# Strassen's seven products in the input projections of three feed-forward layers

## The chip, the cores and the metric

The kernel runs on one core of a Trainium2 chip. The metric is the device time of one execution in microseconds; the lower, the better. Three runs of the kernel before took 3054.96, 3058.57 and 3060.85 us.

## The reference

A network over 512 tokens of width 1024, all in float32. A first block has two layers of mixed recurrent and sparse attention; a second block has two layers, each with a feed-forward network, a mixer, cross-attention to a memory and another feed-forward network. The change is in the feed-forward networks of the second block, four in all:

```
def swiglu_ffn(x, w_in, w_out):
    h = x @ w_in                      # [512, 1024] @ [1024, 5632]
    g, u = jnp.split(h, 2, axis=-1)
    return (jax.nn.silu(g) * u) @ w_out   # [512, 2816] @ [2816, 1024]
...
for i in range(DEPTH):                # 2
    x = layer_norm(a * x + 0.5 * swiglu_ffn(x, ffn_w_in[i, 0], ffn_w_out[i, 0]), ...)
    h = diff_attention(x, ...)  if i == 0 else pool_mixer(x, ...)
    x = layer_norm(a * x + h, ...)
    x = layer_norm(a * x + memory_cross_attention(x, mem, ...), ...)
    x = layer_norm(a * x + 0.5 * swiglu_ffn(x, ffn_w_in[i, 1], ffn_w_out[i, 1]), ...)
```

## The kernel before, in words

The activations stay in the chip's memory: X holds the residual stream with tokens on the partitions, xT (tiles xh and xl) holds it with features on the partitions. Every float32 operand of a matrix product is kept as two parts, an upper one rounded to the matmul's format and a lower one, the rest. A product is three matmuls (upper times upper, upper times lower, lower times upper): `mm3`, L169.

Weights come in units of 512 KB. `units` (L146) loads a unit into a staging tile `wst` (three buffers) with a DMA from SP's queue, ScalarE copies it to the upper part `whi` (L151), and VectorE subtracts that from the staging tile to get the lower part `wlo` (L155). whi and wlo have six buffers each.

`ffn` (L1093) computes one feed-forward layer. The 2816 hidden features are 22 tiles of 128, here called u, worked on in chunks, by default two of 11. For each u there are two units of `w_in`, one for the gate (PSUM tile g, three buffers) and one for the other half (PSUM tile a, two buffers). Each takes 8 row tiles x 3 matmuls with 512 moving columns, the tokens. ScalarE then takes Silu of the gate, VectorE multiplies, ScalarE and VectorE split h into hh and hl (L1121 to L1124). After a chunk comes its share of the output projection, in two halves of 512 output columns, for four tiles of 128 tokens; VectorE adds each result to X (L1138). In the last chunk, for the second half of the columns, the work goes token tile by token tile: matmuls, addition, statistics, layer norm (`ln_tile`, L264, with a power on GpSimd, L198), and the transposition of the tile before into the next xT (`x_T`, L278).

The first two u of a layer are computed in two token halves of 256, since the last token tile of xT comes late: the first half for both, then `flush` (the transposition of the last tile that the phase before left over), then the second half.

The four layers are called at L1623, L1632, L1636 and L1654. The third call asks for chunks of 8, 7 and 7 and carries the pool mixer's steps along. Instructions stand in each engine's queue in an order that the framework fixes when the program is built: it starts from the order of the program text and may put an instruction that it expects to be ready ahead of one that it expects to wait. Waits between engines are by semaphores that it adds.

Of the kernel before, what the change touches and what calls it, by code (L numbers as in the profile page):

```python
# [45 lines left out]
def constants():  # L46
    """Arrays that depend on shapes alone."""
# [38 lines left out]
class Net:  # L86
# [43 lines left out]

    def raw(s, key, *parts):
        """Parts of the weight: the rows r0*128.. (nk tiles of 128) and the columns cols, float32."""
        st = s.w.tile([128, UN], F32, name="wst", bufs=3)
        ap = s.d[key]
        at = 0
        for idx, r0, nk, cols in parts:
            n = nk * len(cols)
            s.specs.setdefault(key, []).append((idx, r0, nk, cols))
            off = s.woff.get(key, 0)
            s.woff[key] = off + 128 * n  # L140
            s.nc.sync.dma_start(st[:, at:at + n], bass.AP(tensor=ap.tensor, offset=ap.offset + off,
                                                          ap=[[n, 128], [1, n]]))
            at += n
        return st, at

    def units(s, key, *parts):  # L146
        """hi and lo of the parts of the weight, each [128, nk, columns]."""
        st, n = s.raw(key, *parts)
        hi = s.w.tile([128, UN], F32R, name="whi", bufs=6)
        lw = s.w.tile([128, UN], F32R, name="wlo", bufs=6)  # L150
        s.nc.scalar.activation(hi[:, :n], st[:, :n], AF.Copy)  # L151
        if s.lo_pool:
            s.nc.gpsimd.tensor_sub(lw[:, :n], st[:, :n], hi[:, :n])
        else:
            s.nc.vector.tensor_sub(lw[:, :n], st[:, :n], hi[:, :n])  # L155
# [5 lines left out]
        return out  # L161

# [11 lines left out]
    def split_ps(s, hi, lo, ps, scale=None):  # L174
        """hi + lo = ps (times a power of two)."""
# [8 lines left out]
    def split_q(s, dst, ps, scale=1.0):  # L184
        """Queries of pairs of heads, feature-major in ps [2 * 64, pairs, tokens], to dst [hi; lo], a head at a time."""
# [6 lines left out]
    def rsqrt(s, v, n, scale, eps, p=128, post=None):  # L192
        """(v * scale + eps) ** -0.5, elementwise on [p, n]."""
# [39 lines left out]
    def to_T(s, src, t, k0, dst):  # L233
        """src [128 tokens, 4 * 128] -> hi / lo [128, k0..k0+3, tokens of tile t]."""
# [6 lines left out]
    def rms_tile(s, t, G, junk):  # L241
        """rmsnorm of X[:, t]."""
        return s.rms_scale(t, G, junk, s.rms_stats(t, junk))
# [20 lines left out]
    def ln_tile(s, t, ST, G, B, parts=1, out=None):  # L264
        """X[:, t] <- layer_norm(sqrt(2) * X[:, t]) with the stats of X in ST."""
# [12 lines left out]
    def x_T(s, t):  # L278
        """X[:, t] feature-major, hi / lo, into s.xT."""
# [4 lines left out]
    def fm(s, key, idx, cols, halves=False, ps=None):  # L284
        """One tile of 128 features, feature-major: [128, 512 tokens] in PSUM."""
# [29 lines left out]
    def tm(s, xT, us, t, ps, ks=None):  # L315
        """Token-major product of the tokens of tile t with the units: [128 tokens, columns] in PSUM."""
# [20 lines left out]
    def open_norm(s, i):  # L337
        """What the first norm of the block takes, on the right side."""
# [167 lines left out]
    def ple(s, i, P):  # L506
        """p @ w_pp / 2 into DRAM, in eight pieces."""
# [26 lines left out]
    def hgrn(s, i, H, L, yh, hf):  # L534
        """The projections; returns the events of the four heads: eight slots a head, and a tail."""
# [262 lines left out]
    def compress(s, i, N, K, gates):  # L798
        """Compressed keys (transposed, twice over the partitions) and block-diagonal values:
# [925 lines left out]
```

## Time and profile before

| | |
|---|---|
| median of three runs | 3058.57 us |
| profiled execution, first to last instruction | 3057.3 us |
| TensorE matmuls busy | 2979.0 us, 15502 instructions |
| VectorE busy | 1656.9 us |
| ScalarE busy | 1144.0 us |
| GpSimd busy | 434.4 us |
| moved by DMA | 296.66 MB |

The profile is one execution on the chip. A busy matmul row counts each matmul from its start to its modelled end, and matmuls overlap, so the pace of a series is read from the starts. A wait is put down to the instruction that ended it last. "PEclk" is the granted clock of TensorE as a share of full speed, "DMA" the mean busy share of the core's 16 DMA engines.

### The profile page before, as it was taken

The page shows a single profiled execution, that of the slowest core. Times are in us where ns is not written, and L with a number is a line of the kernel's source. Part 1 is how long each engine was busy: PE and PEld are TensorE (multiplying, and loading weights), DVE is VectorE, ACT ScalarE, POOL GpSimd, SP SyncE. Part 2 cuts the span into 40 slices and gives each one's busy share as a digit, 9 for nine tenths or more (in the row PEclk, how much of TensorE's full clock was granted, in tenths as well). Part 3 has the DMA queues.
Part 4 walks back from the last instruction along what each step waited for, and adds up shares of the span by engine and source line. Part 5 has one row for each costly group of instructions (what it writes and reads, how often), then busy time and mean ns, then how long its engine had stood idle before and what let it go on. Part 6 is the DMA issues. An engine that isn't in the chain of part 4 may idle for free.

```text
span 3057.3 us, 39959 instructions
## 1 busy us (share of the span) xinstructions
PE 2979.0 (97%) x15502; PEld 2501.9 (82%) x15502; DVE 1656.9 (54%) x2813; ACT 1144.0 (37%) x2063; POOL 434.4 (14%) x555
## 2 busy tenths in 40 slices
PE   8989999989999999999999999999999999999999
PEld 7778778878788888888888888888888888888887
DVE  5676855786765323378775633335333386643334
ACT  6445636545633222245544332222222224332221
POOL 1553500563410000011100000000000040000000
PEclk9999999999999999999999999999999999999999
DMA  5213134113133232231143232324322224132321
GB/s 186 70 55 104 41 128 162 56 61 102 46 121 120 93 100 97 87 107 60 59 157 121 88 104 90 100 90 136 104 97 95 92 75 148 68 118 90 100 91 65
DMA packets 94141, 296.66 MB, mean 97 GB/s; under 512 B 12416, under 2 KB 18048, under 8 KB 93952
## 3 DMA queue, kind: packets, MB, share of 16 engines
q1 hardware_dynamic: 93808, 293.85, 29.5%
q8 instruction: 122, 2.00, 0.3%
q14 instruction: 67, 0.55, 0.1%
q10 hardware_dynamic: 144, 0.26, 0.0%
HBM read 281.49 MB, written 12.58 MB: 96 GB/s over the span
## 4 chain that ended last, share of the span: by engine, by line
PE 82%; DVE 10%; ACT 3%; issue 2%; DMA 2%; POOL 1%; SPq 0%; DVEq 0%; ACTq 0%; POOLq 0%
PE g L167 56%; PE a L167 19%; PE o L167 4%; DVE wlo L155 2%; PE t L237 1%; PE t L1060 1%; POOL rs_y L198 1%; DVE X L274 1%; DVE nb L946 0%; DVE PTl L179 0%; ACT whi L151 0%; DMA wst<-in_w_in 0%; DVE xl L179 0%; DVE AT L645 0%; DVE dqst L190 0%
## 5 line engine op out<-in xcount | busy, mean ns | idle before, releaser
L151 ACT ACTIVATE whi<-wst 128x1024 fp32r<-128x1024 f32 (+1 forms) x478 | 495.9, 1039 | 1173.2 <-PE g L167 453.5
L155 DVE TENSOR_TENSOR wlo<-wst,whi 128x1024 fp32r<-128x1024 f32 (+2 forms) x471 | 572.6, 1220 | 646.5 <-ACT whi L151 627.1
L167 PE MATMUL g<-xh,whi 128*128 128x512 f32 (+1 forms) x1296 | 478.5, 370 | 2.8 <-ACT xh L178 2.2
L167 PE MATMUL g<-xl,whi 128*128 128x512 f32 (+1 forms) x1296 | 476.6, 368 | 1.1 <-DVE xl L179 1.0
L167 PE MATMUL g<-xh,wlo 128*128 128x512 f32 (+1 forms) x1296 | 475.4, 367 | 0.0
L198 POOL TENSOR_TENSOR rs_y<-rs_a,mhalf 128x1 f32<-128x1 f32 (+4 forms) x90 | 100.1, 1113 | 2119.9 <-DVE rs_a L197 2118.4
L167 PE MATMUL g<-whi,xh 128*128 128x512 f32 (+2 forms) x960 | 365.9, 381 | 0.0
L167 PE MATMUL g<-wlo,xh 128*128 128x512 f32 (+2 forms) x960 | 359.5, 374 | 0.8 <-DVE wlo L155 0.8
L167 PE MATMUL g<-whi,xl 128*128 128x512 f32 (+2 forms) x960 | 359.2, 374 | 0.0
L167 PE MATMUL a<-xl,whi 128*128 128x512 f32 (+1 forms) x768 | 286.2, 373 | 0.0
L167 PE MATMUL a<-xh,wlo 128*128 128x512 f32 (+1 forms) x768 | 285.5, 372 | 0.0
L167 PE MATMUL a<-xh,whi 128*128 128x512 f32 (+1 forms) x768 | 285.2, 372 | 0.0
L167 PEld LDWEIGHTS g<-xh,whi 128*128 128x128 f32 x1296 | 244.5, 189 | 43.5 <-ACT xh L178 3.4
L167 PEld LDWEIGHTS g<-xl,whi 128*128 128x128 f32 x1296 | 244.6, 189 | 39.7 <-DVE xl L179 1.5
L167 PEld LDWEIGHTS g<-xh,wlo 128*128 128x128 f32 x1296 | 244.3, 189 | 39.9 <-DVE wlo L155 0.5
L167 PE MATMUL g<-whi,hh 128*128 128x512 f32 x568 | 224.8, 396 | 0.0
L167 PE MATMUL g<-whi,hl 128*128 128x512 f32 x568 | 224.5, 395 | 0.0
L167 PE MATMUL g<-wlo,hh 128*128 128x512 f32 x568 | 224.4, 395 | 0.0
L1122 DVE TENSOR_TENSOR h<-h,a 128x512 f32<-128x512 f32 x88 | 60.6, 688 | 279.8 <-PE a L167 277.7
L167 PEld LDWEIGHTS g<-whi,xl 128*128 128x128 f32 x960 | 182.6, 190 | 30.7
L167 PEld LDWEIGHTS g<-wlo,xh 128*128 128x128 f32 x960 | 183.1, 191 | 29.5 <-DVE wlo L155 1.4
L167 PEld LDWEIGHTS g<-whi,xh 128*128 128x128 f32 x960 | 182.9, 191 | 28.1
(363 smaller groups left out, 4847.4 us busy)
## 6 DMA issues: line engine op xcount, KB each, us to landing
wst<-in_ffn_w_in SPq DMA_DIRECT2D x176, 512.0 KB, 3.5
wst<-in_ffn_w_out SPq DMA_DIRECT2D x80, 512.0 KB, 3.5
wst<-in_w_in SPq DMA_DIRECT2D x64, 512.0 KB, 4.0
wst<-in_xa_wkv SPq DMA_DIRECT2D x32, 512.0 KB, 3.6
wst<-in_da_w_qkv SPq DMA_DIRECT2D x24, 512.0 KB, 3.9
wst<-in_w_out SPq DMA_DIRECT2D x16, 512.0 KB, 3.5
wst<-in_w_pg SPq DMA_DIRECT2D x16, 512.0 KB, 4.4
wst<-in_xa_wq SPq DMA_DIRECT2D x16, 512.0 KB, 4.4
```

The lines of the kernel that those rows point to most:

```text
L151: s.nc.scalar.activation(hi[:, :n], st[:, :n], AF.Copy)
L155: s.nc.vector.tensor_sub(lw[:, :n], st[:, :n], hi[:, :n])
L167: s.nc.tensor.matmul(out, lhsT, rhs, start=start, stop=stop)
L198: nc.gpsimd.tensor_tensor(y, a, s.mhalf[:p].to_broadcast([p, n]), op=OP.pow)
L237: s.nc.tensor.transpose(ps[:, j], src[:, j * 128:(j + 1) * 128], s.ident)
L274: nc.vector.scalar_tensor_tensor(X[:, cs], X[:, cs], rs, B[:, cs], op0=OP.mult, op1=OP.add)
L1060: nc.tensor.transpose(pt[:, j], me["P"][:, j * 128:(j + 1) * 128], s.ident)
L1122: nc.vector.tensor_mul(h, h, pu)
```

## The change

In three of the four layers (both of the first network layer and the last one) the hidden features from u = 2 on are taken in pairs of tiles. For a pair, gate and other half are each 256 columns wide, so `w_in` for it is a 2 x 2 arrangement of blocks (gate or other half, upper or lower 512 rows), and xT is a 2 x 2 arrangement (upper or lower 512 features, first or second 256 tokens). Instead of eight block products there are seven, of sums of blocks, in Strassen's and Winograd's form.

- `sums` makes, once a layer, the four sums of blocks of x on VectorE, and splits them into upper and lower parts (ScalarE and VectorE). It uses three or four of the staging tiles.
- `seven_units` makes the seven weight operands of a pair. Three are blocks as they are. Four are sums: a block is loaded by SP's queue into one of four tiles `sq`, and a second block, or a sum made before, is added by a DMA from GpSimd's queue that accumulates into the tile. s2 takes s3 as its source, s4 takes s2.
- `products` computes the seven products, each 2 column tiles x 4 row tiles x 3 matmuls of 256 moving columns, alternately in g and a, and combines them on VectorE into the gate and the other half.
- All four layers ask for their weights through `need`, which makes them up to five steps ahead of the one in use.
- The default chunks become 6, 6, 6 and 4 instead of 11 and 11. The third layer keeps 8, 7 and 7 and its eight products.

The core of the diff:

```
+    def sums(s, room, F, x):
+        q = {(k, n): tuple(z[:, 4 * k:4 * k + 4, 256 * n:256 * n + 256] for z in x)
+             for k in range(2) for n in range(2)}
+        hi, lo = (room.tile([128, 8, 512], F32R, name=n).rearrange(...) for n in ("xh", "xl"))
+        def full(*key):
+            f = s.stage().rearrange("p (k c) -> p k c", k=4)
+            nc.vector.tensor_add(f, *q[key])
+            return f
...
+        a, b = full(0, 0), full(0, 1)
+        nc.vector.tensor_sub(st[0], a, b)
+        c = full(1, 1)
+        nc.vector.tensor_add(st[1], c, st[0])
+        nc.vector.tensor_sub(st[2], b, c)
+        nc.vector.tensor_sub(st[3], full(1, 0), st[1])
+        for n in (1, 2, 0, 3):
+            nc.scalar.activation(hi[:, n], st[n], AF.Copy)
+            nc.vector.tensor_sub(lo[:, n], st[n], hi[:, n])
+        t = [(hi[:, n], lo[:, n]) for n in range(4)]
+        return q[0, 0], t[1], t[2], t[0], q[1, 0], q[1, 1], t[3]
+
+    def seven_units(s, key, idx, f0, f1, F):
+        def summed():
+            return F.tile([128, UN], F32, name="sq", bufs=4)
...
+        def load(where, st):
+            nc.sync.dma_start(st, where)
+            return st
+        def plus(st, src):
+            nc.gpsimd.dma_start(st, src, accum_op=OP.add)
+            return st
+        def u0():
...
+            me["s3"] = plus(load(me[1, 0], summed()), me[0, 0])
+            me["s1"] = plus(load(me[1, 0], summed()), me[1, 1])
+            me["s2"] = plus(load(me[1, 1], summed()), me["s3"])
+            me["s4"] = plus(load(me[0, 1], summed()), me["s2"])
+            return split(load(me[0, 0], s.stage()))
+        return [u0, lambda: split(me["s2"]), lambda: split(me["s3"]), lambda: split(me["s1"]),
+                lambda: split(load(me[0, 1], s.stage())), lambda: split(me["s4"]),
+                lambda: split(load(me[1, 1], s.stage()))]
+
-    def ffn(s, i, j, want_T, out=False, after=None, chunks=(11, 11)):
+    def ffn(s, i, j, want_T, out=False, after=None, chunks=(6, 6, 6, 4), seven=False, room=None):
...
+            def need(n, ahead=5):
+                while len(made) < min(n + 1 + ahead, len(steps)):
+                    made.append(steps[len(made)]())
+                return made[n]
...
+            def products(at, hh, hl, u):
+                sg = P.tile([128, 2, 2, 256], F32, name="sg", bufs=1)
+                hr = P.tile([128, 2, 512], F32, name="h", bufs=1)
+                h = hr.rearrange("p j (n c) -> p n j c", n=2)
+                def mul(n, ps):
+                    w = need(at + n)
+                    b = ps().rearrange("p (j c) -> p j c", j=2)
+                    for z in range(2):
+                        for k in range(4):
+                            s.mm3(b[:, z], tuple(x[:, k, z * 128:(z + 1) * 128] for x in w),
+                                  (t7[n][0][:, k], t7[n][1][:, k]), k == 0, k == 3)
+                    return b
+                p1, U2, U3 = (P.tile([128, 2, 256], F32, name=n, bufs=1) for n in ("p1", "U2", "U3"))
+                nc.scalar.activation(p1, mul(0, s.g), AF.Copy)
+                nc.vector.tensor_sub(U2, mul(1, s.a), p1)
+                nc.vector.tensor_add(U3, mul(2, s.g), U2)
+                b = mul(3, s.a)
+                nc.vector.tensor_sub(h[:, 1], U3, b)
+                nc.vector.tensor_sub(U2, U2, b)
+                nc.vector.tensor_add(sg[:, 0], mul(4, s.g), p1)
+                nc.scalar.activation(sg[:, 0], sg[:, 0], AF.Silu)
+                nc.vector.tensor_sub(sg[:, 1], mul(5, s.a), U2)
+                nc.scalar.activation(sg[:, 1], sg[:, 1], AF.Silu)
+                nc.vector.tensor_add(h[:, 0], mul(6, s.g), U3)
+                nc.vector.tensor_mul(h, h, sg)
+                nc.scalar.activation(hh[:, u:u + 2], hr, AF.Copy)
+                nc.vector.tensor_sub(hl[:, u:u + 2], hr, hh[:, u:u + 2])
...
                     s.flush()
+                    if seven:
+                        t7 = s.sums(room or P, P, xT)
+                for u, by7, at in inner:
+                    if by7:
+                        products(at, hh, hl, u - u0)
...
-                    s.ffn(0, 0, True)
+                    s.ffn(0, 0, True, seven=True)
-                    s.ffn(0, 1, True)
+                    s.ffn(0, 1, True, seven=True, room=s.xt)
-                    s.ffn(1, 1, False, out=True)
+                    s.ffn(1, 1, False, out=True, seven=True, room=s.xt)
```

## Rows read from the trace of the kernel before

**Rows 1.** Busy time of each engine over the span.
```profile
PE 2979.0 (97%) x15502; PEld 2501.9 (82%) x15502; DVE 1656.9 (54%) x2813; ACT 1144.0 (37%) x2063; POOL 434.4 (14%) x555
```

**Rows 2.** Chain of waits that ended last, shares by engine.
```profile
PE 82%; DVE 10%; ACT 3%; issue 2%; DMA 2%; POOL 1%; SPq 0%; DVEq 0%; ACTq 0%; POOLq 0%
```

**Rows 3.** Busy time in stretches of the second changed layer; last PEclk, DMA share, GB/s.
```profile
1872.00:1935.00 63.00, 63.00 (x272) 50.78 (x271) 19.06 (x21) 13.68 (x14) 0.00 (x0) 1.00 0.31 96
1935.00:2050.00 115.00, 115.00 (x504) 94.33 (x503) 39.06 (x43) 32.70 (x42) 0.00 (x0) 1.00 0.29 94
```

**Rows 4.** Waits of PE in each changed layer: us, times, longest.
```profile
PE g L167 <- ACT xh L178: 1.2, 1, 1.2
PE g L167 <- ACT xh L178: 0.3, 1, 0.3
PE g L167 <- ACT xh L178: 0.2, 1, 0.2
```

**Rows 5.** PE timeline, input projection: first matmuls of two successive tiles; start, duration.
```profile
1961.12 0.39 PE L167 MATMUL g<-xh,whi 128*128 128x512 f32 x1
...
1966.61 0.39 PE L167 MATMUL a<-xh,whi 128*128 128x512 f32 x1
```

**Rows 6.** PE timeline, first token halves: first matmuls of two successive tiles.
```profile
1746.46 0.28 PE L167 MATMUL a<-xh,whi 128*128 128x256 f32 x1
...
1749.29 0.28 PE L167 MATMUL g<-xh,whi 128*128 128x256 f32 x1
```

**Rows 7.** PE timeline, key projection: two matmuls that are 24 apart.
```profile
1590.07 0.28 PE L167 MATMUL g<-mTh,whi 128*128 128x256 f32 x1
...
1592.91 0.28 PE L167 MATMUL g<-mTh,whi 128*128 128x256 f32 x1
```

**Rows 8.** Groups of instructions over the span: count, busy us, mean ns, idle before.
```profile
L155 DVE TENSOR_TENSOR wlo<-wst,whi 128x1024 fp32r<-128x1024 f32 x445 | 553.3, 1248 | 635.7 <-ACT whi L151 616.2 <-PE a L167 11.0
L151 ACT ACTIVATE whi<-wst 128x1024 fp32r<-128x1024 f32 x452 | 478.3, 1060 | 1111.7 <-PE g L167 449.8 <-PE o L167 277.4 <-PE a L167 267.7
...
L1122 DVE TENSOR_TENSOR h<-h,a 128x512 f32<-128x512 f32 x88 | 60.6, 688 | 279.8 <-PE a L167 277.7 <-ACT h L1121 2.1
...
L1121 ACT ACTIVATE h<-g 128x512 f32<-128x512 f32 x88 | 50.9, 579 | 0.4 <-PE g L167 0.4
```

**Rows 9.** DMA from 1935 to 2050 us: packets, MB, share; issues, KB, landing.
```profile
q1 hardware_dynamic: 3024, 10.75, 28.7%
...
wst<-in_ffn_w_in SPq DMA_DIRECT2D x13, 512.0 KB, 3.4
```

**Rows 10.** DMA issues of 512 KB elsewhere: count, size, median us to landing.
```profile
X<-in_x SPq DMA_DIRECT2D x8, 512.0 KB, 6.9
...
xbuf<-X SPq DMA_DIRECT2D x8, 512.0 KB, 2.6
```

**Rows 11.** GpSimd and VectorE side by side (timeline); lower halves, ns min/median/max.
```profile
3043.95 1.28 DVE L273 SCALAR_TENSOR_TENSOR X<-X,mv,G 128x1024 f32<-128x1024 f32 x1
...
3044.17 1.46 POOL L198 TENSOR_TENSOR rs_y<-rs_a,mhalf 128x1 f32<-128x1 f32 x1 [6.24 <-DVE rs_a L197]
...
3051.88 0.92 POOL L198 TENSOR_TENSOR rs_y<-rs_a,mhalf 128x1 f32<-128x1 f32 x1 [6.25 <-DVE rs_a L197]
...
L155 DVE TENSOR_TENSOR wlo<-wst,whi x471: 681/1225/2294, 6.0 to 3022.3; 128x1024 fp32r<-128x1024 f32 x148, 128x512 fp32r<-128x512 f32 x7, 128x840 fp32r<-128x840 f32 x2
```

**Rows 12.** Timeline at the start of the second changed layer: SP, DVE, PE.
```profile
1751.16 0.33 SPq L204 DMA_DIRECT2D G<-in_ln_g  x1
...
1756.21 1.29 DVE L179 TENSOR_TENSOR xl<-t,xh 128x512 fp32r<-128x512 f32 x2 [5.07 <-ACT xh L178]
...
1767.89 0.39 PE L167 MATMUL g<-xl,whi 128*128 128x512 f32 x1
```

**Rows 13.** DVE timeline at the end of the last layer: evacuations of two tiles, last norm.
```profile
3042.18 0.69 DVE L1138 SCALAR_TENSOR_TENSOR X<-g,X 128x512 f32<-128x512 f32 x1 [2.93 <-PE g L167]
...
3049.88 0.69 DVE L1138 SCALAR_TENSOR_TENSOR X<-g,X 128x512 f32<-128x512 f32 x1 [2.93 <-PE g L167]
...
3052.97 1.41 DVE L274 SCALAR_TENSOR_TENSOR X<-X,rs_y,B 128x512 f32<-128x512 f32 x2
```

More of the change, by code (lines that the diff above doesn't have):

```diff
@@ L129, in load_const, with stage @@
         return ct
+    def stage(s):
+        return s.w.tile([128, UN], F32, name="wst", bufs=3)
     def raw(s, key, *parts):
-        st = s.w.tile([128, UN], F32, name="wst", bufs=3)
-        ap = s.d[key]
+        st = s.stage()
         at = 0
@@ new lines, in seven_units, with summed, split, part @@
+    def seven_units(s, key, idx, f0, f1, F):
+        nc = s.nc
+        me = {}
+        def summed():
+            return F.tile([128, UN], F32, name="sq", bufs=4)
+        def split(st):
+            return tuple(x.rearrange("p (k c) -> p k c", k=4) for x in s.halves(st))
+        def part(i, k):
+            f = (f0, f1)[i]
+            return s.place(key, idx, 4 * k, 4, list(range(f, f + 256)))
+        def load(where, st):
[5 more added lines that the diff above has]
+        def u0():
+            for i in range(2):
+                for k in range(2):
+                    me[i, k] = part(i, k)
+            me["s3"] = plus(load(me[1, 0], summed()), me[0, 0])
[6 more added lines that the diff above has]
+                lambda: split(load(me[1, 1], s.stage()))]
@@ L1098, in ffn, with plain_in @@
             xT = s.xT
+            steps, made = [], []
+            def need(n, ahead=5):
+                while len(made) < min(n + 1 + ahead, len(steps)):
+                    made.append(steps[len(made)]())
+                return made[n]
+            def plain_in(u):
+                at = len(steps)
+                for c0 in (0, FF):
+                    f0 = c0 + u * 128
+                    steps.append(partial(s.unit, "ffn_w_in_2", (i, j), 0, 8, list(range(f0, f0 + 128))))
+                return at
@@ new lines, in seven_in, with rows @@
+            def seven_in(u):
+                at = len(steps)
+                steps.extend(s.seven_units("ffn_w_in_2", (i, j), u * 128, FF + u * 128, P))
+                return at
+            def rows(u0, nu, c):
+                at = len(steps)
+                for r0 in range(0, nu, 2):
+                    steps.append(partial(s.unit, "ffn_w_out_2", (i, j), u0 + r0, min(2, nu - r0),
+                                         list(range(c * 512, (c + 1) * 512))))
+                return at
@@ L1099, in ffn @@
+            plan = []
             u0 = 0
             for nu in chunks:
+                inner = []
+                u = u0
+                while u < u0 + nu:
+                    if seven and u >= 2:
+                        inner.append((u, True, seven_in(u)))
+                        u += 2
+                    else:
+                        inner.append((u, False, plain_in(u)))
+                        u += 1
+                plan.append((u0, nu, inner, [rows(u0, nu, c) for c in range(2)]))
+                u0 += nu
@@ L1128, in ffn @@
                 for c in range(2):
[L1129 to L1134 removed]
+                    nunits = -(-nu // 2)
                     def evac(t, ps):
@@ L1140, in evac, with row @@
                             nc.vector.bn_stats(ST[:, t, c], x)
+                    def row(k):
+                        wh, wl = need(outs[c] + k // 2)
+                        return wh[:, k % 2], wl[:, k % 2]
                     if last and c:
+                        us = [row(k) for k in range(nu)]
                         for t in range(4):
@@ L1455, in mem_kv @@
         for z in range(2):
-            st = s.w.tile([128, UN], F32, name="wst", bufs=3)
+            st = s.stage()
             nc.sync.dma_start(st, s.d["memT"][z])
```

74 lines of the change are left out of this document (38 added, 36 removed).

## The prediction

> **What bounds the kernel now.** I began with the busy times of the whole span: the matmul row of TensorE is busy 97% of it, VectorE 54%, ScalarE 37%, GpSimd 14% [rows 1]. The chain of waits says the same by cause: 82% of the time is the matmul engine's own work, 10% VectorE's, 2% a DMA's [rows 2]. A mean over stages hides what one stage is like, so the next view was busy time by stretch inside a changed layer. In an out-projection (1872 to 1935 us) and in an input projection (1935 to 2050 us) TensorE is busy all the time at the full granted clock (1.00, the 2.4 GHz level), VectorE for about a third of the time, GpSimd not at all, and the DMA engines have a share of 0.29 to 0.31 [rows 3]. The matmul engine's list of waits over each of the three changed layers has one entry: 1.2, 0.3 and 0.2 us [rows 4]. So a microsecond taken from TensorE there is a microsecond off the span, as long as the operands still come in time; this prediction is about that condition.
>
> **TensorE: seven products for eight.** A busy matmul row overlaps its neighbours, so its price is read from start to start. A feature tile of the input projection is 24 matmuls of 512 columns; one begins at 1961.12 us and the next one at 1966.61: 5.49 us, 228.8 ns each [rows 5]. The first tiles of the layer are computed in token halves, 24 matmuls of 256 columns, which is the shape of the new products (2 column tiles x 4 row tiles x 3): 1746.46 to 1749.29 us, 2.83 us [rows 6]. Two units cost four of the former now, 21.96 us, and seven of the latter afterwards, 19.81 us: 2.15 us less, not the eighth (2.75 us) that the count of products promises, since half the columns cost 0.515 of the time. Ten pairs in each of three layers give 30 x 2.15 = **64.5 us**. Bounds: by the key projection, another run of 256-column matmuls, 24 take 2.84 us [rows 7], so 62 us; at an exact eighth, 82 us. I take the row of the same layer.
>
> **VectorE and ScalarE in the products.** VectorE has per pair seven lower halves at 1.25 us, seven combinations of 512 elements with PSUM at 0.69 us, and the product and lower half of h, now 1024 wide, at 1.25 us: 8.75 + 4.8 + 2.5 = 16.1 us of 19.81 (before, 7.8 of 21.96). ScalarE: eight passes of 1024 at 1.06 us and three of 512 at 0.58: 10.2 us [rows 8]. Both lie beside TensorE. A PSUM bank is wanted again three or more products (8.5 us) after it was filled, and weights are made five steps ahead into six buffers, so I cost this at nothing. If that cover goes, every VectorE instruction that comes late costs up to 1.25 us in each pair.
>
> **DMA.** A pair had four 512 KB loads; it gets seven, and four accumulates. In the input projection the weight queue took 28.7% of 16 engines over 115 us for 10.75 MB, 20.5 loads: 1.61 us of all engines for one, 3.4 us from issue to landing [rows 9]. The trace has no accumulate. It can hardly take less than a load of its size, 1.61 us; at most it is a load, a load of the destination and a store, 4.8 us. I take 3.2 us, two reads. A pair then asks 7 x 1.61 + 4 x 3.2 = 24.1 us of the DMA engines against 19.81 us of TensorE, more than it has. But a full chunk holds three pairs (59.4 us) and an out-projection of 144 matmuls (33.6 us at 7.70/33 us each, [rows 13]) that asks only six loads, 9.7 us: 82 us of 93. The next chunk's first pair can load beneath the out-projection.
>
> The landing matters more than the rate: s2 needs s3 to have landed, s4 needs s2, and all four stand in GpSimd's one queue. Two landings in a row must fit into a pair's 19.81 us. Bounds for one landing: 3.4 us as a plain load, and 13.8 us, twice the slowest load of this size [rows 10]. I take 7 us, twice the nearest row; 14 us fit. The new wait is ScalarE's upper half of a summed weight: behind it in ScalarE's queue stand p1, the Silu passes and h, behind those VectorE's combinations, and TensorE waits for the banks that they free. For slips I put 6 us in all (18 pairs aren't the first of their chunk).
>
> The request five steps ahead moves each unit's load on SP's queue, its ScalarE pass and its VectorE pass to before the matmuls of five earlier units, in the layer between too. With six weight buffers and three staging buffers, as before, they can't run earlier than a buffer comes free, which is what ScalarE already waits for; I cost that at nothing, and at one pass (1.25 us) where it lands in front of an evacuation.
>
> One rule of the Trainium skill speaks against putting these on GpSimd. The rows first: GpSimd's rs_y takes 1.46 us when it starts beside a 1.28 us VectorE instruction, and 0.92 us where VectorE's work is cut into halves; a lower half on VectorE, 1.23 us as a rule, takes up to 2.29 us [rows 11]. The SBUF — State Buffer page, "Who interferes with whom", says that a VectorE instruction with two SBUF inputs and a GpSimd instruction that reads SBUF exclude each other, and that a DMA issued from GpSimd can be starved while its descriptors wait. By that rule, if it holds for these issues, each would come up to one VectorE instruction (1.25 us) later, a landing 8.3 us instead of 7, and two of them, 16.5 us, still fit; the sum stays and the slower case below gains chance.
>
> **Start of a layer.** The sums of x add 12 VectorE instructions (15 us) and four ScalarE passes. They wait for the last token tile, whose lower halves are done at 1757.5 us; the token halves of the first two units keep TensorE until 1767.89 [rows 12], the first product needs no sum, so the second is due at 1770.7. Until then VectorE owes six of the 12 (7.5 us), four weight halves (5 us) and the first two units' four instructions (2.8 us): done at 1772.8, 2 us late. The sums also borrow the three weight staging buffers, one of which may be held by a weight that waits for a buffer of the first units. The chain of weight sums starts about when the queue is free (1751.16, [rows 12]): 3.4 + 7 + 7 us is 1768.6, just in time. I put 3 us a layer, **9 us** (0 to 24).
>
> **More chunks.** Four chunks for two make eight passes of the out-projection for four. Matmuls are the same; 16 more evacuations at 0.69 us lie beside them. I put 0.5 us for each new change of pass, **6 us** (0 to 12).
>
> **Tail.** The last pass goes token tile by token tile. A tile now lasts 33 matmuls, 7.70 us [rows 13]; with a chunk of four it is 12, 2.8 us, while its evacuation and norm ask 3.8 us of VectorE. So VectorE is late next: after the last layer 4 x 3.8 us + 0.8 of latency from the first tile's end, against 3 x 2.8 us of matmuls, 7.6 us behind the last matmul where it is now 4.5 (3049.88 to 3054.4, [rows 13]): +3 us. In the first layer, whose successor needs all four tiles, I put 2 us; in the second 11.3 us of first halves cover it. **5 us**.
>
> **Sum.** -64.5 + 6 + 9 + 6 + 5 = -38.5 us. The profiled execution has a span of 3057.3 us and the median of the runs is 3058.57 (1.3 us lie around the span): **3020 us**.
>
> **Rivals.** (a) VectorE in the way: at 16.1 of 19.81 us it is 81% full and its instructions wait on ScalarE, PSUM and landings in a fixed order; one 1.25 us instruction late in each pair is 37.5 us, which leaves 3058 us. For it: the share. Against it: three products of PSUM slack, and that TensorE hardly waits in these layers now.
> (b) The accumulates' landings become the bound. If one takes 12 us, two make a pair's period 24 us, 4.2 us over TensorE's 19.81, in the 18 pairs that no out-projection covers: +75 us, **3095 us**, slower than before. It decides from a landing of 11.0 us, where 18 x 2.1 us eat the 38.5. For it: the DMA engines are asked for more than 100% inside a pair, and loads in front of an accumulate lengthen it; x at the start of the span, with a full queue, took 6.9 us for a plain load [rows 10]. Against it: the slack beneath each out-projection, and GpSimd's idle queue.
> (c) The products don't come at the 256-column pace. At 168 matmuls in 21.96 us, 130.7 ns each, the gain is nil and the overheads of 26 us are left: 3085 us. Against it: two runs of that shape at 118 ns.
>
> **Chances.** A difference under 0.2% (6.1 us) can't be told from none. Forecast 0.58, with its own range of 2990 (every cover holds) to 3040; (a) 0.14, spread over 3040 to 3065, 0.08 of it faster, 0.05 same, 0.01 slower; (b) 0.20, slower; (c) 0.08: 0.04 faster, 0.01 same, 0.03 slower. Faster 0.70, same 0.06, slower 0.24. Range 2990 to 3075: the likeliest case, (a), (c) for the most part and the near end of (b).
>
> **What would show it.** Right: 24-matmul products at 2.83 us from start to start, TensorE without waits inside a chunk, accumulates landing in 5 to 9 us, the first weight sum of a layer ready before the second product, some 3 us more behind the last matmul. Wrong: TensorE or ScalarE waiting on the summed weights in the second and third pair of a chunk (b); TensorE waiting for PSUM with VectorE busy throughout (a); 256-column matmuls beyond 120 ns apart (c). The layer between, computed as before, should keep its time.

## The result, and the profile after

The changed kernel takes 3131.93 us (median of 4 runs, 3125.69 to 3139.08), the kernel before 3057.38 us (3054.96 to 3060.85): a ratio of 1.0245, interval 1.0231 to 1.0259, **75 us slower** where 38.5 us faster was forecast. The profiled execution has a span of 3130.0 us, 72.7 more than before.

The page's busy times, after; they answer to [rows 1]:

```profile
PE 2959.1 (95%) x17662; PEld 2587.4 (83%) x17662; DVE 1960.8 (63%) x3131; ACT 1258.7 (40%) x2159; POOL 539.2 (17%) x675
```

TensorE is busy 19.9 us less than before, and idle 170.9 us (3130.0 - 2959.1) where it was 78.3: +92.6. So the products saved something, and waits ate it. The matmul engine's waits over the whole span (us in total, times, longest):

```profile
PE a L176 <- ACT xh L1126: 39.9, 3, 15.1
PE g L176 <- DVE h L1255: 30.1, 9, 4.4
PE a L176 <- ACT whi L168: 14.7, 4, 6.1
...
PE g L176 <- DVE sg L1251: 7.1, 4, 3.0
```

Where there was one short entry a layer [rows 4] there are now two large ones. Three times, once a changed layer, the second product waits for the first sum of x (L1126 splits it). Nine times, at three chunk ends in each of three layers, the out-projection waits for a PSUM bank: the one that the last product of the pair just made has filled and that the addition into h (L1255) empties. Of the four waits for whi, one of 6 us stands in the kernel before as well; the other three, 2.7 to 3.0 us, come in the second pair of each changed layer. Four stretches of the changed kernel (us; busy times and counts of PE, PEld, DVE, ACT, POOL; granted clock; DMA share; GB/s): the start of the first changed layer, a chunk's end, the out-projection after it, and the middle of a chunk in the second layer:

```profile
985.00:995.00 10.00, 2.90 (x12) 2.60 (x13) 10.00 (x10) 4.71 (x5) 0.00 (x0) 0.50 0.23 78
...
1125.00:1150.00 25.00, 21.00 (x132) 18.97 (x132) 14.89 (x17) 8.44 (x10) 1.75 (x2) 0.86 0.90 250
1150.00:1180.00 30.00, 30.00 (x137) 24.44 (x136) 11.79 (x14) 6.36 (x6) 2.63 (x3) 1.00 0.55 136
...
1910.00:1930.00 20.00, 20.00 (x170) 20.00 (x169) 14.28 (x15) 8.84 (x10) 2.63 (x3) 1.00 0.93 250
```

The last row is the change as it was meant: 170 matmuls of 256 columns in 20 us, 117.6 ns each, nothing waited for. The first is the start: TensorE runs 2.9 of 10 us, and when it runs again it has the 1.2 GHz level (0.50). The two in the middle show the DMA engines at 0.90 while a pair is made and at 0.55 beneath the out-projection, where [rows 3] have 0.31. The page's DMA queues (packets, MB, share of 16 engines) and issues (count, KB, median us to landing):

```profile
q0 software_dynamic: 17280, 62.92, 11.2%
...
sq<-in_ffn_w_in SPq DMA_DIRECT2D x120, 512.0 KB, 5.1
wst<-in_ffn_w_out SPq DMA_DIRECT2D x86, 512.0 KB, 5.7
...
sq<-in_ffn_w_in POOLq DMA_DIRECT2D x60, 512.0 KB, 8.1
sq<-sq POOLq DMA_DIRECT2D x60, 512.0 KB, 6.9
```

Queue q0 holds the 120 accumulates alone: 0.112 x 3130 / 120 = 2.92 us of all 16 engines for each. In the median one lands 6.9 or 8.1 us after its issue, and plain loads land later too: 5.1 and 5.7 us where [rows 9] have 3.4. The median hides the worst: of the 90 loads of w_out 28 take more than 8 us to land, up to 12.7; in the kernel before the slowest takes 4.6.

**The start, instruction by instruction.** The timeline of the first changed layer on four engines:

```profile
960.84 2.50 SPq L1148 DMA_DIRECT2D sq<-in_ffn_w_in  x4
963.21 1.21 DVE L1112 TENSOR_TENSOR wst<-xh,xl 128x1024 f32<-128x1024 f32 x1
974.42 0.88 POOL L1152 DMA_DIRECT2D sq<-sq  x1 [4.33 <-DMA sq<-in_ffn_w_in]
980.14 2.95 ACT L168 ACTIVATE whi<-sq 128x1024 fp32r<-128x1024 f32 x3 [8.11 <-DMA sq<-sq]
980.41 0.86 POOL L1152 DMA_DIRECT2D sq<-sq  x1 [5.11 <-DMA sq<-sq]
981.23 3.50 DVE L169 TENSOR_TENSOR wlo<-sq,whi 128x1024 fp32r<-128x1024 f32 x3 [10.41 <-ACT whi L168]
...
985.78 1.22 DVE L1120 TENSOR_TENSOR sq<-wst 128x1024 f32<-128x1024 f32 x1
```

VectorE makes a first operand of the sums of x at 963.21 and then has next to nothing to do until 981.23. The differences of x (L1120) begin at 985.78, right after the upper and lower halves of the weight sums are made. Their target is named sq: besides the staging tiles, the sums of x take the four tiles in which the first pair's weight sums lie, so x has to wait for the accumulates to land.

**A chunk's end.** SP issues four w_out loads from 1126.50 on, among the loads and accumulates of the next chunk's first pair, and the first three need 7.1, 10.4 and 9.9 us to land. ScalarE waits for two of them, VectorE for ScalarE's upper half, and the last combinations of the pair stand behind that in VectorE's queue:

```profile
1126.50 9.89 SPq L140 DMA_DIRECT2D wst<-in_ffn_w_out  x4
...
1133.72 1.06 ACT L168 ACTIVATE whi<-wst 128x1024 fp32r<-128x1024 f32 x1 [6.06 <-DMA wst<-in_ffn_w_out]
1138.75 1.06 ACT L168 ACTIVATE whi<-wst 128x1024 fp32r<-128x1024 f32 x1 [3.97 <-DMA wst<-in_ffn_w_out]
1139.71 0.61 ACT L1252 ACTIVATE sg<-sg 128x512 f32<-128x512 f32 x1
...
1139.84 1.23 DVE L169 TENSOR_TENSOR wlo<-wst,whi 128x1024 fp32r<-128x1024 f32 x1 [3.21 <-ACT whi L168]
...
1142.72 0.69 DVE L1255 TENSOR_TENSOR h<-g,U 128x512 f32<-128x512 f32 x1
...
1143.45 0.79 PE L176 MATMUL g<-whi,hh 128*128 128x512 f32 x1 [4.00 <-DVE h L1255]
```

So the weights that hold TensorE up here are not summed ones but plain blocks of w_out. At each of the nine ends ScalarE has waited for a w_out load in the 13 us before, the longest time 2.2 to 9.8 us. The wait of TensorE costs more than its 4.00 us: ahead of it the 512-column matmuls start 0.23 us apart, behind it 0.43 us apart until 1149.6.

**The tail** is nearly as forecast. VectorE, last evacuation and end of the last norm; compare [rows 13]:

```profile
3118.87 0.69 DVE L1287 SCALAR_TENSOR_TENSOR X<-g,X 128x512 f32<-128x512 f32 x1
...
3125.34 1.41 DVE L283 SCALAR_TENSOR_TENSOR X<-X,rs_y,B 128x512 f32<-128x512 f32 x2
```

The norm ends 7.9 us after the start of the last evacuation, where it was 4.5.

### The profile page after: what moved, and what is told of

Read it like the earlier page. It is cut to its first block, busy times and chain, and to the rows that moved or that the text cites. A ratio compares the mean times of both kernels' runs of the same rounds, so it can differ in the third digit from the quotient of the medians.

```text
span 3130.0 us, 45448 instructions
## 1 busy us (share of the span) xinstructions
PE 2959.1 (95%) x17662; PEld 2587.4 (83%) x17662; DVE 1960.8 (63%) x3131; ACT 1258.7 (40%) x2159; POOL 539.2 (17%) x675
## 3 DMA queue, kind: packets, MB, share of 16 engines
q0 software_dynamic: 17280, 62.92, 11.2%
## 5 line engine op out<-in xcount | busy, mean ns | idle before, releaser
L168 ACT ACTIVATE whi<-wst 128x1024 fp32r<-128x1024 f32 (+2 forms) x442 | 461.6, 1047 | 746.5 <-PE g L176 261.9
L176 PE MATMUL g<-xh,whi 128*128 128x256 f32 (+1 forms) x1776 | 564.8, 319 | 2.8 <-ACT xh L1126 1.7
L176 PE MATMUL g<-xl,whi 128*128 128x256 f32 (+1 forms) x1776 | 559.9, 316 | 0.7 <-DVE xl L188 0.6
L176 PE MATMUL g<-xh,wlo 128*128 128x256 f32 (+1 forms) x1776 | 559.8, 315 | 0.3 <-DVE wlo L169 0.3
L176 PE MATMUL a<-xh,whi 128*128 128x256 f32 (+1 forms) x1008 | 307.2, 305 | 48.5 <-ACT xh L1126 39.9
L176 PE MATMUL a<-xh,wlo 128*128 128x256 f32 (+1 forms) x1008 | 306.4, 304 | 2.0 <-DVE wlo L169 2.0
L176 PE MATMUL a<-xl,whi 128*128 128x256 f32 (+1 forms) x1008 | 305.7, 303 | 0.0
L168 ACT ACTIVATE whi<-sq 128x1024 fp32r<-128x1024 f32 x120 | 124.7, 1056 | 342.6 <-PE o L176 122.1
L169 DVE TENSOR_TENSOR wlo<-sq,whi 128x1024 fp32r<-128x1024 f32 x120 | 146.0, 1223 | 183.6 <-ACT whi L168 183.6
L176 PE MATMUL g<-whi,hh 128*128 128x512 f32 x547 | 222.8, 407 | 37.3 <-DVE h L1255 30.1
L176 PEld LDWEIGHTS a<-xh,whi 128*128 128x128 f32 x1008 | 196.7, 195 | 56.0 <-ACT xh L1126 40.5
```

Of the source, the lines that this page charges most:

```text
L169: (s.nc.gpsimd if s.lo_pool else s.nc.vector).tensor_sub(lw[:, :n], st[:, :n], hi[:, :n])
L176: s.nc.tensor.matmul(out, lhsT, rhs, start=start, stop=stop)
```

## Experiments

All ratios are to the kernel before, on the same chip, with 95% intervals; times of different experiments, which did not all run on one chip, are compared by their medians, and the kernel before has medians of 3056.7 to 3059.1 us there. A layer's length runs from the last transposed x to the end of its last norm.

### e1: the sums of x in buffers of their own

```
-        st = [summed() for _ in range(4)]            # the ring "sq" of the weight sums
...
+        v = F.tile([128, 2, 2, 256], F32, name="sg", bufs=1)...   # a-b, then +c, then d-that, in place
...
+        nc.vector.tensor_sub(b, b, c)                             # in its staging tile
```

> The sums of x are made in place in the layer's sg tile and a staging tile, instead of in the four buffers that the weight sums use too; same products, same loads and accumulates. Theory S (start of the layer: the sums of x cannot begin before the first pair's weight sums have landed and been halved, since they borrow their buffers): the three stalls of 15.1, 12.7 and 12.2 us on xh shrink to under 4 us each, with them some 3 us a layer of lower granted clock: 3131.9 - 30 - 9 = about 3093 us (3080 to 3105). Theory V (the DMA engines' volume: 24 to 27 us of transfers asked per 20 us pair): the start just waits for the weight sums instead, within 10 us of 3132. Theory C (more chunks and the shorter last one): unchanged, 3132.

Measured: 3104.42 us (ratio 1.0158, 1.0143 to 1.0173), 27.5 us less than the changed kernel. Its waits of TensorE:

```profile
PE g L176 <- DVE h L1258: 31.0, 9, 5.3
PE a L176 <- ACT xh L1116: 12.3, 2, 6.8
```

The stalls on x fall from 39.9 to 12.3 us in two starts; the third start, in the first layer, now waits 5.2 us for the first summed weight instead. These three, 5.2 to 6.8 us, were expected under 4. The nine waits at the chunk ends stay. The loan of the buffers is shown; it is a little over a quarter of the 104 us that e2 puts on the accumulates.

### e2: no accumulates

```
-            nc.gpsimd.dma_start(st, src, accum_op=OP.add)
             return st
```

> The four accumulating DMAs of each pair are left out (so four of the seven weights are plain blocks, not sums); loads, halves, products and combinations stay. Theory V: DMA share inside a pair falls from 0.9-1.0 to about 0.6, w_out loads land in under 4.5 us, TensorE's waits at the chunk ends go too: all of the extra 100 us over the forecast, 3020 to 3035. Theory S: only the start is mended, 3131.9 - 40 - 9 = about 3083 (3070 to 3095), the 30 us of waits ahead of the out-projections stay. Theory C: 3125 or more.

Measured: 3027.64 us (0.9908, 0.9892 to 0.9925). Page and waits of TensorE:

```profile
PE 2928.2 (97%) x17662; PEld 2565.1 (85%) x17662; DVE 1969.1 (65%) x3131; ACT 1262.8 (42%) x2159; POOL 434.8 (14%) x555
...
wst<-in_ffn_w_out SPq DMA_DIRECT2D x86, 512.0 KB, 3.6
```

```profile
PE a L176 <- ACT xh L1126: 11.1, 3, 4.3
```

So 104.3 us hang on the accumulates, and not on the three extra loads a pair: they stayed, and loads land in 3.6 us. The kernel leaves the weight sums out, so four of its seven weights are plain blocks; TensorE has the same matmuls to do. By the spans, the 106.5 us are 75.6 of idle time and 30.9 of busy time: the same 17662 matmuls are busy 2959.1 us in the changed kernel. A wait on TensorE is paid for a second time, in matmuls at the lower clock behind it, as at 1143.45.

### e3: the chunks without the seven products

```
-                    s.ffn(0, 0, True, seven=True)      # and the two others
+                    s.ffn(0, 0, True)
```

> Chunks of 6, 6, 6 and 4 feature tiles and the request five steps ahead, as in the changed kernel, but all input projections by the eight plain products, no sums. It times the chunking and tail alone. Prediction's terms: 3057.4 + 6 + 5 = 3068 (3060 to 3080). Theories S and V: under 3080, since the loss is elsewhere. Theory C: 3100 or more.

Measured: 3071.58 us (1.0045, 1.0030 to 1.0060): chunks, tail and the request five steps ahead cost 14.9 us together where the prediction has 11. TensorE is busy 2986.7 us here and 2928.2 in e2, so the seven products save 58.5 us of it.

### e4: the same accumulates, no landing waiting for a landing

```
-            me["s2"] = plus(load(me[1, 1], summed()), me["s3"])
-            me["s4"] = plus(load(me[0, 1], summed()), me["s2"])
+            me["s2"] = plus(load(me[1, 1], summed()), me[0, 0])
+            me["s4"] = plus(load(me[0, 1], summed()), me[0, 0])
```

> The same number and size of loads and accumulates, but the third and fourth accumulate of a pair add a block from DRAM instead of the sum that the first one left (other weights are computed): no landing waits for another landing. Theory L (it is the chain of landings, two or three in a row): the start gains one to two landings of 6 to 7 us, 3 x 7 to 3 x 13, and the second pair of a layer (ScalarE waited 17 us) comes on time: 3085 to 3110. Theory V (volume): all of DRAM's reads stay, within 12 us of 3132. Theory S: one landing less a layer, about 3112.

Measured: 3134.41 us (1.0251, 1.0235 to 1.0266), as slow as the changed kernel. Without the chain of landings, which the prediction thought the critical thing, nothing is gained: in the first layer ScalarE begins on the first summed weight 19.2 us after SP's first load of the pair, with the chain 19.3. The four accumulates are then in flight together, and the landing of one takes longer, 8.4 us in the median.

### e5 and e6: two or all four weight sums on GpSimd

From e1. The third and fourth sum are added on GpSimd from blocks that are loaded anyway (e5, shown here); or all four (e6):

```
-            me["s2"] = plus(load(me[1, 1], summed()), me["s3"])
-            me["s4"] = plus(load(me[0, 1], summed()), me["s2"])
...
+            me["t11"] = load(me[1, 1], s.stage())        # also the seventh product's weight
...
+            me["s2"] = both(me["t11"], me["s3"])         # nc.gpsimd.tensor_add into a tile of "sq"
+            me["t01"] = load(me[0, 1], s.stage())        # also the fifth product's
+            me["s4"] = both(me["t01"], me["s2"])
```

> From e1: s2 and s4 are added on GpSimd from two blocks that are loaded anyway, so two accumulates (2 x 2.92 us of the 16 DMA engines) and two loads (2 x 1.6) of each pair go: 13.9 us of transfers for 19.8 us of matmuls instead of 22.9 (and w_out loads besides). Theory V (the DMA engines cannot bring a pair in time): TensorE's waits at the chunk ends and the low-clock stretches go, as in e2: 3015 to 3035. Rival P (GpSimd's additions, 2.4 to 2.7 us each as the seven lower halves on GpSimd of the kernel before, keep VectorE from its own): VectorE 16.1 + 5 = 21 us a pair, 1.3 over TensorE's pace in 30 pairs: 3055 to 3065. Rival B (buffers and order, not volume, make them late): 3095 to 3110 as e1.

> From e1: all four weight sums are added on GpSimd from four plain loads: 6.4 us of transfers a pair, as the kernel before has, no accumulating DMA; GpSimd 4 x 2.4 to 2.7 = about 10 us a pair. Theory V without P: 3015 to 3030, the same as e5 since volume no longer counts. Rival P: VectorE 16.1 + 10 = 26 us a pair: 6 us over TensorE's pace in each, 3015 + 180 = about 3190, and in any case later than e5. Rival B: 3095 or more.

Measured: e5 3057.33 us (0.9998, 0.9989 to 1.0008), e6 3059.60 us (1.0005, 0.9996 to 1.0014). e5's number is the one that rival P named, but not for P's reason, and e6, as fast, is where no theory had it. In e5, a window of a chunk and the waits of TensorE tell why:

```profile
1800.00:1900.00 100.00, 100.00 (x704) 93.50 (x704) 72.92 (x71) 40.52 (x45) 22.71 (x14) 1.00 0.61 160
```

```profile
PE g L176 <- ACT xh L1116: 42.1, 3, 16.9
```

In this stretch TensorE never stops, at the full clock, with a DMA share of 0.61, and the waits at the chunk ends are gone from its list, in the same order of work: that is theory V's answer. But the three starts are back at 14 us, because the blocks of the first weight sums now stay in the three staging tiles that the sums of x want: the same mistake with another ring (e9). Rival P is half right: VectorE does get slower. Lower halves of summed weights (busy us, mean ns), first in e6, then in e1:

```profile
L169 DVE TENSOR_TENSOR wlo<-sq,whi 128x1024 fp32r<-128x1024 f32 x120 | 199.8, 1668 | 81.3 <-ACT whi L168 80.9
```

```profile
L169 DVE TENSOR_TENSOR wlo<-sq,whi 128x1024 fp32r<-128x1024 f32 x120 | 146.2, 1223 | 175.5 <-ACT whi L168 175.5
```

VectorE's busy time is 150 us higher than in e1 (2112.4 against 1962.1), 1.25 us for each of the 120 additions, and TensorE does not notice.

### e7 and e8: each pair's out-projection behind the next pair's products

e7 keeps all four accumulates and spreads them; e8 does the same from e6:

```
+            for p in range(n):                       # 11 pairs of feature tiles
+                seq.append(("in", p, ...))           # the products of pair p
+                if p:
+                    seq.append((0, [p - 1], ...))    # then pair p-1, first 512 columns
+                    if p - 1 < n - 3:
+                        seq.append((1, [p - 1], ...))    # and the second 512
+            ...                                      # the last three pairs' second 512 by token tile
```

> From e1: same DMAs, sums and products, but the out-projection of each pair (48 matmuls of 512 columns, 11.2 us) stands behind the next pair's products, so that transfers are asked evenly: 7 x 1.61 + 4 x 2.92 + 2 x 1.61 = 26.2 us of the DMA engines for every 31.0 us of TensorE, in place of 69 us for 59.4 us and then 9.7 for 33.6; the second halves of the last three pairs' out-projection stand at the end token tile by token tile. VectorE gets 68 more evacuations a layer at 0.69 us. Theory V in its burst form: most of e1's loss goes, 3025 to 3055. If the mean load of 85% is already too much (landings grow with it, whatever the order): 3080 to 3110. Rival B: 3095 to 3110.

> e6 and e7 together: weight sums on GpSimd and the out-projection pair by pair. Theory V: both remedies answer the same cause, so it is within 10 us of the better of the two, less the tail's 3 x 2 us: 3010 to 3030. Rival P: VectorE has 16.1 + 5.5 + 10 = 31.6 us in 31.0, so e6's loss mostly goes: 3030 to 3060.

Measured: e7 3049.75 us (0.9969, 0.9960 to 0.9979), 54.7 us under e1 with the same transfers. A stretch of it:

```profile
1800.00:1900.00 100.00, 98.54 (x663) 90.98 (x664) 75.95 (x87) 38.71 (x43) 12.30 (x14) 0.98 0.85 223
```

At a mean DMA share of 0.85 TensorE is busy 98.5% of the time, and only 5 of the 90 loads of w_out take more than 8 us to land. So these bytes can be brought in time when they are asked for evenly. The edit changes more than the spreading: the order of work and the last pass (three pairs in place of two) differ too. e8 took 3141.41 us (1.0269, 1.0253 to 1.0285), which no theory had. Its waits of TensorE over the span, then of SP's queue from 1800 to 2100 us:

```profile
PE g L176 <- DVE h L1412: 70.1, 27, 4.8
```

```profile
SPq L1151 <- DVE wlo L169: 185.0, 34, 18.2
SPq L140 <- DVE wlo L169: 106.3, 16, 14.7
```

From 1800 to 1900 us the DMA share is 0.29, so the bytes are not the bound, and SP waits for tiles: two of three staging tiles hold a pair's blocks until its fifth and seventh weight are halved, and the w_out loads now stand between the pairs in the same ring. But SP waits nearly as long in e6 (176.8 and 90.1 us in the same window), which has no such loss. What differs is ScalarE, which waits 40.1 us there for GpSimd's sums and in e6 13.4. That the buffers are the bound is a guess; no run with more of them was made, and e8's loss stays open.

### e9, e10, e11, e15: the starts and the chunk order

From e5. e9 builds the sums of x in the tiles sg, h and p1-U2; e10 is e9 with another chunk order; e11 is e10 with both products of plain blocks first, and with no weights asked for ahead while the two plain units are computed, so that the sums of x stand before the first pair's weights; e15 is e11 with the changed kernel's chunks.

```
+        v = full((0, 0), flat(F.tile(..., name="sg", bufs=1)))     # e9
+        b = full((0, 1), flat(F.tile(..., name="pU", bufs=1)))
+        c = full((1, 1), F.tile(..., name="h", bufs=1)...)
...
-    chunks=(6, 6, 6, 4)                                            # e10, e11
+    chunks=(4, 6, 6, 6)
...
-        return q[0, 0], t[1], t[2], t[0], q[1, 0], q[1, 1], t[3]   # e11, e15
+        return q[0, 0], q[1, 0], t[1], t[2], t[0], q[1, 1], t[3]
...
+    first[u] = [s.fm_part(need(at + z, 5 - 5 * seven), ps()) for z, ps in enumerate((s.g, s.a))]   # e11, e15
```

> From e5 (two adds on GpSimd): three of the four sums of x are now made in the layer's own sg, h and a p1-U2 tile, so that they don't borrow the staging tiles in which the blocks of the first weight sums lie; nothing else. Theory S' (e5's 42.1 us of waits on xh at the layers' starts are a second loan of buffers): the three stalls of 14 us shrink to 5 us each (first weight sum ready 5 us after the first product) and the clock stays up: 3057.3 - 27 - 6 = 3024 (3010 to 3035). If the starts wait for the weight sums' landings anyway: 3045 to 3060.

> From e9: chunks of 4, 6, 6 and 6 feature tiles instead of 6, 6, 6 and 4. The last pass then has 18 matmuls of 512 columns a token tile, 4.2 us, over the 3.8 us that its evacuation and norm ask of VectorE; e3 measured chunks and tail together at 14.9 us. Theory T (most of that is the short last chunk): 2 to 3.5 us less a layer, 6 to 10 us under e9. If it is the number of chunks: within 4 us of e9.

> From e10: the two products that need neither a weight sum nor... of x among the first (A00 by x00, then A01 by x10) come first, the sums of x stand ahead of the first pair's weight halves, and T is made in the U tile. The first weight sum is due 2.8 us later: TensorE's stalls at the three starts fall by 2.8 to 5 us each, 8 to 15 us under e10: about 3005 (2995 to 3015).

> e11 with the changed kernel's chunks of 6, 6, 6 and 4. Its first chunk has two pairs behind the plain units, so that the out-projection does not begin on the pair just finished. If e10's loss against e9 (11.8 us) is that, as the waits on hl and hh in its first out-projection say: about 12 us under e11, 3031 (3025 to 3036), the fastest of all. If it is something else in the order of the chunks: 3038 or more.

Measured: e9 3038.68 us (0.9933, 0.9918 to 0.9948), e10 3050.49 (0.9971, 0.9960 to 0.9982), e11 3043.17 (0.9947, 0.9931 to 0.9964), e15 3038.23 (0.9933, 0.9917 to 0.9950). e9's largest wait of TensorE in the changed layers, and the one that e10 adds in the first 4-tile chunk of its second layer:

```profile
PE g L176 <- ACT h L1237: 21.7, 3, 7.9
```

```profile
PE g L176 <- DVE hl L1273: 1.9, 1, 1.9
```

e9 gains 18.7 us over e5 by the second loan alone, less than the 33 expected: 7 us a start are left. There TensorE waits for a bank that the Silu of a plain unit (L1237) empties; in the first layer that Silu stands in ScalarE's queue behind upper halves of the first pair's weights, the first of which waited 7.5 us for GpSimd's sum. The order of e11 takes 7.3 us off e10, just short of the 8 to 15. e10 is a miss of the wrong sign: 11.8 us slower than e9. A first chunk with one pair makes its out-projection wait for the pair just finished. But undoing that in e15 gave 4.9 us, not the 12 expected, and the waits seen add up to some 6 us, so a part of e10's loss stays open. e9 and e15, equal within their intervals, are the fastest kernels here that compute the layers in full (e2 and e13 leave the weight sums out), some 19 to 20 us under the kernel before.

### e12: all four accumulates with everything else mended

e11 with the changed kernel's accumulates and loads in place of GpSimd's additions.

> e11 with all four accumulates of the changed kernel in place of GpSimd's two additions (and seven loads): only the transfers differ, 22.9 us a pair in place of 13.9. Theory V: inside the chunks it stays as late as e1, so 45 to 75 us over e11: 3050 to 3080. If the changed kernel's loss was the starts and the tail alone: within 12 us of e11.

Measured: 3098.22 us (1.0128, 1.0110 to 1.0145), 55 us over e11: as theory V had the difference.

### e13 and e14: copies that nobody waits for

```
-            nc.gpsimd.dma_start(st, src, accum_op=OP.add)
+            for _ in range(1):                    # e14: range(2)
+                nc.gpsimd.dma_start(s.dr.tile([128, UN], F32, name="dd", bufs=8), st)
```

> From the changed kernel: each accumulate is replaced by one plain copy of the 512 KB tile that it would have added to, out to DRAM, on the same GpSimd queue after the same load (the weight sums are left out, nobody reads the copies). Transfers asked by a pair: 11 x 1.6 = 17.7 us of 19.8, e2 has 11.3, the changed kernel 22.9. Theory V (volume): between, near e2 as long as a pair still fits: 3030 to 3060. Theory A (the accumulation as such): the same as e2, 3022 to 3034, since no summed weight lands late.

> As e13 with two such copies for each accumulate: 15 x 1.6 = 24 us asked in 19.8 us, about what the changed kernel asks, with no sum that anyone waits for. Theory V: loads land late as they do there: 3085 to 3135. Theory A: within 15 us of e2, 3022 to 3043.

Measured: e13 3033.45 us (0.9922, 0.9907 to 0.9937), e14 3059.60 us (1.0006, 0.9996 to 1.0015). The queue and the copies of e14, and its waits:

```profile
q0 software_dynamic: 34560, 125.84, 10.7%
...
dd<-sq POOLq DMA_DIRECT2D x240, 512.0 KB, 7.1
```

```profile
PE g L176 <- DVE h L1256: 12.8, 6, 4.7
PE g L176 <- DVE sg L1252: 11.4, 3, 4.6
```

e13 lies in the ranges of both theories and decides nothing. By share of the DMA engines e14's copies weigh nearly what the accumulates do (10.7% of 3060 us, 1.36 us each, against 11.2% of 3130). They cost 32 us over e2, at the chunk ends as well (e13's half of that costs 6). So it is neither theory alone. By subtraction, 32 of the 104 us come with the volume as such, by late loads, which is rather too much for it: SP's next load into a tile does wait for the copy, 24.8 us in the first layer. The other 72 come only where somebody waits for the sums. Of these e1 accounts for 27.5, the start.

No run divides the other 45, but the waits of TensorE in e1 show where they arise. At the chunk ends it loses 36.0 us (31.0 for h, 5.0 for sg), behind late w_out loads, where e14 loses 24.2. In the second pair of each layer it loses 11.5 us for a bank (U, L1253), and in the first layer, where I followed it, ScalarE has just waited 10.4 us for the landing of a weight sum; e14 has no such wait of TensorE. The lower clock behind the waits adds to both. e4 says that unlinking the accumulates doesn't help, e7 that spreading the transfers does.

## Why the prediction was wrong, point by point

Layer lengths, us, and the medians:

| kernel | first | second | third | median |
|---|---|---|---|---|
| before | 359.4 | 361.4 | 357.8 | 3057.4 |
| after | 389.9 | 383.9 | 384.2 | 3131.9 |
| e1 own buffers | 378.2 | 379.2 | 374.0 | 3104.4 |
| e2 no accumulates | 353.7 | 352.6 | 348.3 | 3027.6 |
| e3 chunks alone | 364.6 | 369.1 | 363.3 | 3071.6 |
| e7 spread | 361.1 | 359.8 | 354.3 | 3049.8 |
| e9 two adds, own start | 358.0 | 356.0 | 349.8 | 3038.7 |

The stretch between the second and the third changed layer, the layer with eight products in it, kept its time: 575.8 us, before 577.7.

- **TensorE, -64.5 us: right in the pace.** 117.6 ns a matmul in the trace against 118 forecast; e2 against e3 gives 58.5 us less busy time. Rival (c) is out.
- **VectorE and ScalarE beside the products, 0: right as far as load goes.** In e5 VectorE is busy 73% of a stretch with TensorE at 100%. Rival (a) is out: no wait of TensorE came from VectorE's load. But the fixed order of ScalarE and VectorE, named there as a risk, is how a late load reached TensorE.
- **DMA, +6 us: the step that failed, about 77 us** (3104.4, the start mended, less e2's 3027.6; e12 less e11 gives 55). The prices of an accumulate were good: 2.92 us of engine time against 3.2, median landings of 6.9 and 8.1 us against 7, within the 5 to 9 named as a sign of being right. What was made of them was wrong, three times. First, the excess of 24.1 us asked in 19.81 was averaged over chunk and out-projection. But the four sq tiles hold one pair and come free while that pair's products run, so the next pair's transfers run there and then. The first pair of the next chunk, meant to load beneath the out-projection, loads from 1117.62 on, 20 us before the out-projection begins, and its last accumulate lands at 1144.5. The share is 0.90 from 1125 to 1150, and 0.55 beneath the out-projection. Second, plain loads were left at their 3.4 us. In such bursts 28 of the 90 loads of w_out took more than 8 us, and ScalarE's upper halves of these plain blocks, not of the summed weights, are what the nine chunk ends wait behind: 30.1 us, and more by the clock. Third, "two landings in a row must fit into a pair's 19.81 us" left out the load ahead of them: 5.1 + 8.1 + 6.9 = 20.1 us to s2, before it is halved. It looked like the cause, but e4, without that chain, was as slow; with less volume in the same order (e2, e5) the waits at the chunk ends go, and with the same volume spread (e7) TensorE's waits for h and sg fall from 36.0 us in e1 to 12.9.
- **Rival (b) had the side and the reason right, more asked of the DMA engines than a pair has, but neither the price nor the place**: it ends at 3095 with landings of 12 us and was to decide from 11.0. It came at medians of 7 to 8 us, TensorE waited mostly at the chunk ends behind w_out loads, and where nobody waited for a sum (e14) a third of the cost came all the same.
- **Start of a layer, +9 us: failed.** The prediction lists the loan of the staging tiles and overlooks that of the sq tiles, in the same function of the diff. e1 gives 27.5 us back, and TensorE still waits 5.2 to 6.8 us in each start. The chain of weight sums is late too: in the first layer 19.3 us from the first load to the landing of s2, against 17.4 forecast, since the load, issued with three others, took 6.6 us and not 3.4.
- **More chunks and tail, +11 us: a little low**; 14.9 in e3. The last norm ends 7.9 us after the last evacuation begins, 7.6 were forecast.
- **Not priced at all: the clock behind a stall.** 30.9 us between the changed kernel and e2 are the same matmuls running longer, with 0.50 to 0.86 granted around the stalls where [rows 3] have 1.00.

From kernel to kernel the 75 us divide so: +14.9 from the kernel before to e3 (chunks and tail), -43.9 from there to e2 (the products; TensorE is busy 58.5 us less, and part of that goes again in the starts, where e2 waits 11.1 us for x), +76.8 to e1 (the accumulates beside the rest) and +27.5 to the changed kernel (the loan).

## What to carry to other kernels

Ask of each new tile ring who else takes tiles from it, at the moment when both need it: two loans of buffers here cost 27 and 19 us. Compare the transfers with the engine time in each stretch between two points where a buffer must come free, not over a whole loop; a mean share of 0.85 did little harm when it was even (e7), and the same transfers cost over 50 us more in bursts. Plain loads that share a burst land late as well. A wait put on TensorE was dearer here than its length, since the matmuls behind it ran slower for a while.

## What the runs showed of the hardware

- An accumulating DMA of 512 KB into SBUF took 2.92 us of all 16 DMA engines, a copy of that size out to DRAM 1.36 (e14), a plain load 1.61 [rows 9].
- A plain load of 512 KB landed in 3.4 us at a share of 0.29 [rows 9], and three of the four issued from 1126.50 on, at 0.90, took 7.1 to 10.4 us.
- GpSimd's addition of 128x1024 took 2.35 to 3.45 us and made VectorE 1.25 us busier each time (e6), about one of its own instructions. A lower half of a summed weight took 1.22 us in the mean away from an addition (80 of them) and 2.57 beside one (40), up to 3.47; a combination that reads a PSUM bank took 0.68 either way. The Trainium skill, SBUF — State Buffer, "Who interferes with whom", has the two exclude each other; this trace agrees for additions. Whether DMAs issued from GpSimd were held up by VectorE, which the prediction weighed, no run separated.
- After some 15 us of near idleness TensorE came back at 0.50, the 1.2 GHz level, and had 0.95 in the next 10 us (995 to 1005).
